# First stage of a two-layer attention kernel: a modulation third in two column halves, products by feature halves, and the shift applied as columns are formed

## The chip, the cores and the metric

The kernel runs on one core of a Trainium2 chip. The metric is the device time of one execution in microseconds (us). Five engines work side by side, each through its own queue in order: TensorE (PE; PEld is its weight load), VectorE (DVE), ScalarE (ACT), GpSimd (POOL) and SyncE (SP), whose queue issues nearly all transfers.

## The reference, cut to what matters

1024 image tokens and 256 context tokens of 1024 features go through two attention layers. What the change touches is the head of the first layer: normalise, modulate by a condition vector, project.

```python
def _modulate(x, cond, norm_g, w_ada, b_ada):
    mod = jax.nn.silu(cond) @ w_ada + b_ada
    shift, scale, gate = jnp.split(mod[:, None, :], 3, axis=-1)
    return rmsnorm(x, norm_g) * (1.0 + scale) + shift, gate

h, gate = _modulate(x, c, norm_g, w_ada, b_ada)
hc, gate_c = _modulate(xc, c_ctx[None, :], norm_g, w_ada, b_ada)
qa, ka, va, qb, kb, vb, g = _split(h @ w_in, EVEN_SPLITS)
```

Everything is float32. The kernel multiplies at that precision by splitting each operand into a high part in a reduced format (fp32r) and the remainder, and adding three products (`mm3`: high x high, high x low, low x high).

## The kernel before, in words

`h` holds the modulated tokens turned to features x tokens: 8 feature tiles (`kt`) of 128 features, 1280 tokens, as a high and a low tile (`hE`). Tokens come in three chunks, `CHUNKS`: 0 to 511 (first tokens), 512 to 1023 (second tokens), 1024 to 1279 (context). The modulation matrix `w_ada_e` has three thirds of 1024 columns: shift (0), scale (1), gate (2). `ada_third` loads a third as eight 128x1024 tiles (`wada`, 512 KB each), multiplies `sil` with them in four column groups into one PSUM tile, copies that (`mrow`), turns it and adds the bias into `modT`.

The first stage, from the kernel's start to the mark "e1":

- The first four token tiles are loaded (`load_x`), normalised (`norm_rows`), turned and copied unscaled (`raw_cols`), while the scale third is loaded and multiplied; `scale_cols` then forms the high and low columns of the first tokens, scaled and not yet shifted. The `issue_after` blocks hold those instructions behind the split of the first projection weight.
- `load_ws` loads four projection tiles (`first = (4, 0, 1, 2)`) one after another through one buffer `wraw` and splits each (ACT the high part, DVE or POOL the remainder).
- `products` multiplies the four weights, one after the other, with the first tokens (`proj_fm`, 24 matmuls of 512 columns each) into four PSUM tiles `early`, and is advanced a little at a time (`Filler`, `FILL_S0`, `FILL_S1`) between the shift third and `cols_scaled` of the second tokens, which are scaled and not yet shifted.
- `bias` multiplies the shift with the four weights, so that `finish` can add it to products of unshifted columns, rotate them (`rope_split`: DVE, POOL, ACT) and store them (`store_hl`).
- `qk_first` makes the same products of the second tokens, again weight by weight, while the context's columns are formed with shift (`h_cols`) and `shift_cols` rebuilds the first tokens' columns with shift.
- `qk_ctx` makes the context's products and those of two further weights, `w5` (`va_part`) and `w3` (`proj_spill`), for the context and the first tokens, while `shift_cols` rebuilds the second tokens' columns.

Behind the mark "e1" come `va_part` and `proj_spill` of the remaining chunk (the second tokens), the split of four weights (`W2`), `va_tm`, and then `v_spill`, whose products fill TensorE while the other thirds are multiplied.

Instructions are traced in the order of the code; a scheduler at compile time sets each engine's own order from that, from the data and from free buffers. At run time every engine goes through its order, and a waiting instruction holds all behind it. `t_ps()` gives two PSUM buffers for turned tiles, `mm_ps()` two, `s_ps()` three, `pv_ps()` one; with `mm_state["wide"]` on, `mm_ps()` also takes from `s_ps()`. Token tiles (`xt`) have six buffers.

Of the kernel before, what the change touches and what calls it, by code (L numbers as in the profile page):

```python
# [18 lines left out]
P = 128  # L19
D = 1024  # L20
# [20 lines left out]
ADA_E1, ADA_BUFS = ((0, 2), (1, 0), (1, 1), (1, 2)), 6  # L41
# [4 lines left out]
H_ACT, FILL_S, W_AHEAD, FILL_S0, FILL_S1, FILL_S2, FILL_S3, FILL_S4, SH_V, HF_BUFS = 2, 1.6, 3, 3.0, 1.4, 8.0, 1.2, 3.0, 3, 2  # L46
# [50 lines left out]
def body(nc, tc, I, out, dbg=None):  # L97
# [325 lines left out]
    def ada_third(wt, name, layer, third, step=1):  # L423
        acc = s_ps()[:, :256]
        for k0 in range(0, NK, step):
            ws_ = []
            for kt in range(k0, k0 + step):
                w = wt.tile([P, D], F32, tag="wada", name="wada", bufs=ADA_BUFS)
                SY.dma_start(w, I[name][kt * P:(kt + 1) * P, third * D:(third + 1) * D])
                ws_.append((kt, w))  # L430
# [18 lines left out]
        else:  # L449
            A.copy(row, acc)  # L450
            if (layer, third) == (0, 1):
                yield 0.0
# [13 lines left out]

    def gate_load(dst, i):
        SY.dma_start(dst, GROW[i:i + 1].to_broadcast([P, D]))

    def norm_rows(tp, xs):  # L470
        n = len(xs)
        ss = tiny.tile([P, n], F32, tag=f"ss{n}", name="ss")
        for i, x in enumerate(xs):
            junk = tp.tile([P, D], BF16, tag="junk", name="junk", bufs=1)
            A.activation(junk, x, AF.Square, accum_out=ss[:, i:i + 1])
        r = rstd_of(ss, n, D)
        for i, x in enumerate(xs):
            V.tensor_scalar(x, x, r[:, i:i + 1], None, ALU.mult)
# [17 lines left out]

    def raw_cols(xns, raw):
        n = len(xns) * P
        for kt in range(NK):
            ps = t_ps()  # L500
            for b, xn in enumerate(xns):
                T_.transpose(ps[:, b * P:(b + 1) * P], xn[:, kt * P:(kt + 1) * P], ident)
            (V.tensor_copy if kt % 2 else A.copy)(raw[:, kt, :n], ps[:, :n])

    def scale_cols(raw, layer, j, c0, n, h):
        for kt in range(NK):
            gs = modT[layer][:, 8 + kt, j:j + 1]
            hi, lo = h[0][:, kt, c0:c0 + n], h[1][:, kt, c0:c0 + n]
            A.activation(hi, raw[:, kt, c0:c0 + n], AF.Identity, scale=gs)
            V.scalar_tensor_tensor(lo, raw[:, kt, c0:c0 + n], gs, f32(hi), ALU.mult, ALU.subtract)  # L510
# [42 lines left out]
    with ExitStack() as st:  # L553
# [3 lines left out]
        sr, sc = ExitStack(), ExitStack()  # L557
        sp = pool(sc, "start", 2, side="left")
        raw0 = pool(sr, "raw0", 1, side="left").tile([P, NK, 512], F32, name="raw0")
# [26 lines left out]
        lo_cycle["engs"] = [V, G]  # L586
        first = (4, 0, 1, 2)
        ws, xs = [], []

        def load_ws():  # L590
            j = len(ws)
            raw = wsp.tile([P, D], F32, tag="raw", name="wraw")
            SY.dma_start(raw, I["w_e"][first[j]])
            a = A.copy(wst[0][:, j], raw)
            v = (G if j % 2 else V).tensor_tensor(wst[1][:, j], raw, f32(wst[0][:, j]), ALU.subtract)
            ws.append([w[:, j:j + 1] for w in wst])
            return a.ins, v.ins

        rows = [load_x(b) for b in range(4)]
        norm_rows(xp, rows)  # L600
        raw_cols(rows, raw0)
        ada = ada_third(sp, "w_ada_e", 0, 1)
        for _ in range(NK + 1):
            next(ada)
        split = load_ws()
        run(ada)
        with tc.issue_after(split[0]), tc.issue_after(split[1]):
            scale_cols(raw0, 0, 0, 0, 512, h)
        for i in range(4):
            if len(ws) < min(i + 1, W_AHEAD):  # L610
                load_ws()
            xs.append(load_x(4 + i))
        sr.close()
        early = [mm_ps(), mm_ps(), s_ps(), pv_ps()]

        def products():
            for j in range(4):
                yield from proj_fm(ws[j], h, 0, 512, ps=early[j])
                yield 1.28

        prods = Filler(products())
        prods(FILL_S0)
        norm_rows(xp, xs)
        cols = cols_scaled(xs, 0, 0, 512, h)
        for i, _ in enumerate(ada_third(sp, "w_ada_e", 0, 0)):
            if i % 2 and len(ws) < 4:
                load_ws()
            prods(FILL_S1)
            next(cols, None)
        run(cols)  # L630
        sc.close()
# [34 lines left out]
        def qk_first():  # L666
            for j in range(4):
                ps = yield from proj_fm(ws[j], h, 512, 512)
                finish(j, ps, 512, 512)
                yield 1.28  # L670
# [9 lines left out]
        def qk_ctx():  # L680
            for j in range(4):
                yield from proj_chunk(tp, ws[j], h, S, L, cs, QK[first[j]])
            for c in (2, 0):
                yield from va_part(c)
                yield from proj_spill(tp, w3, h, CHUNKS[c:c + 1], cs, QK[3])

        mm_state["wide"] = True
        bias()
        prods.drain()
        for j in range(4):  # L690
# [3 lines left out]
        side(FILL_S2)  # L694
# [16 lines left out]
    with ExitStack() as st:  # L711
# [15 lines left out]
        with ExitStack() as sq:  # L727
            tp = pool(sq, "q3", 2, side="left")
            run(va_part(1))
# [879 lines left out]
```

## Time and profile before

| | us |
|---|---|
| median of 3 runs | 1656.78 (1656.08 to 1659.83) |
| the profiled execution | 1659.88 |
| its span in the trace | 1658.1 |
| TensorE busy | 1583.4 of the span |
| DVE, ACT, POOL busy | 1085.6, 777.8, 540.2 |

The profiled execution has 1.8 us outside its span. A matmul's busy time overlaps its neighbour's in the trace, since they are pipelined: what one costs is the distance from its start to the next one's start.

### The profile page before, as it was taken

How to read it: one execution, taken by the hardware profiler on the slowest of the kernel's cores; microseconds unless marked ns; L12 is line 12 of the kernel's file. 1: busy time of each engine (PE TensorE's matmuls, PEld its weight loads, DVE VectorE, ACT ScalarE, POOL GpSimd, SP SyncE). 2: the span in 40 equal slices, each digit the busy share in tenths (PEclk: the TensorE clock that was granted, in tenths of full speed). 3: DMA queues.
4: the chain of work that ended last, by engine and by line, in shares of the span. 5: the costliest groups of instructions: out<-in, count | busy, mean ns of one | idle time of the engine just before them, and what ended most of it. 6: DMA issues, size and time to landing. Idle time of an engine off the chain costs nothing. (4 is left out here: it accounts for less than half of the span.)

```text
span 1658.1 us, 26760 instructions
## 1 busy us (share of the span) xinstructions
PE 1583.4 (95%) x9250; PEld 1330.5 (80%) x9250; DVE 1085.6 (65%) x2954; ACT 777.8 (47%) x1580; POOL 540.2 (33%) x713
## 2 busy tenths in 40 slices
PE   6989999999998999999899999999999999999997
PEld 3677768888877878888677797989888888888886
DVE  4674128878759887887777546343587756665576
ACT  5443006766646566556333323222476655554421
POOL 0365024555444333323333202120243414322211
PEclk9989999999999999999999999999999999999999
DMA  7547663242262333222853623557755436321452
GB/s 287 180 115 247 242 200 119 84 141 90 71 219 96 97 109 113 89 87 77 255 190 114 186 61 105 187 178 240 224 167 174 131 118 196 100 81 64 140 191 83
DMA packets 147231, 242.40 MB, mean 146 GB/s; under 512 B 10236, under 2 KB 93976, under 8 KB 144920
## 3 DMA queue, kind: packets, MB, share of 16 engines
q1 hardware_dynamic: 142184, 227.32, 43.6%
q10 hardware_dynamic: 4576, 11.54, 1.8%
q0 software_dynamic: 336, 1.84, 0.3%
q8 instruction: 73, 1.20, 0.3%
q14 instruction: 62, 0.51, 0.1%
HBM read 162.91 MB, written 77.74 MB: 145 GB/s over the span
## 5 line engine op out<-in xcount | busy, mean ns | idle before, releaser
L304 PE MATMUL mmps<-hE,whi 128*128 128x512 f32 (+1 forms) x408 | 148.7, 364 | 1.3 <-DVE gg L396 1.3
L218 POOL TENSOR_TENSOR wlo<-wraw,whi 128x256 fp32r<-128x256 f32 x120 | 92.4, 803 | 174.0 <-ACT whi L251 168.9
L306 PE MATMUL mmps<-hE,wlo 128*128 128x512 f32 (+1 forms) x408 | 146.4, 359 | 0.0
L305 PE MATMUL mmps<-hE,whi 128*128 128x512 f32 (+1 forms) x408 | 146.3, 359 | 0.0
L914 ACT ACTIVATE sB_t<-sB_t,mB 128x1280 f32<-128x1280 f32 (+1 forms) x80 | 95.5, 1194 | 58.9 <-DVE sB_t L407 49.4
L906 PE MATMUL sps<-kb,qb 128*128 128x512 f32 (+1 forms) x416 | 107.4, 359 | 5.8 <-DVE sB_t L407 3.1
L924 POOL TENSOR_SCALAR sB_t<-sB_t,cB 128x256 f32<-128x256 f32 x84 | 38.6, 479 | 157.9 <-DVE cB L920 76.3
L407 DVE TENSOR_SCALAR_CACHE_REDUCE sB_t<-sps,mB 128x512 f32<-128x512 f32 (+1 forms) x128 | 78.4, 613 | 12.4 <-PE sps L906 9.4
L304 PEld LDWEIGHTS mmps<-hE,whi 128*128 128x128 f32 x408 | 77.3, 190 | 11.4 <-issue 2.1
L306 PEld LDWEIGHTS mmps<-hE,wlo 128*128 128x128 f32 x408 | 77.2, 189 | 10.0 <-issue 0.8
L305 PEld LDWEIGHTS mmps<-hE,whi 128*128 128x128 f32 x408 | 77.2, 189 | 9.2 <-issue 0.8
L906 PEld LDWEIGHTS sps<-kb,qb 128*128 128x128 f32 x416 | 68.8, 189 | 18.3 <-DVE sB_t L407 7.1
L1442 POOL TENSOR_SCALAR sM_t<-sM_t,sM 128x1280 f32<-128x1280 f32 x32 | 43.4, 1357 | 117.5 <-DVE sM L1441 116.6
L218 POOL TENSOR_TENSOR rot<-rot,csE 128x256 f32<-128x256 f32 x52 | 41.3, 814 | 112.1 <-DVE rot L331 108.4
L1340 POOL TENSOR_SCALAR sD_t<-sD_t,sD 128x640 f32<-128x640 f32 (+1 forms) x64 | 50.0, 800 | 81.7 <-DVE sD L1337 49.9
L305 PE MATMUL mmps<-hO,whi 128*128 128x512 f32 (+1 forms) x192 | 74.5, 388 | 1.7 <-POOL hO L214 1.6
L304 PE MATMUL mmps<-hO,whi 128*128 128x512 f32 (+1 forms) x192 | 75.4, 393 | 0.0
L784 ACT ACTIVATE sA_t<-sA_t,mA 128x640 f32<-128x640 f32 (+2 forms) x80 | 59.6, 745 | 31.8 <-DVE sA_t L407 29.2
L306 PE MATMUL mmps<-hO,wlo 128*128 128x512 f32 (+1 forms) x192 | 74.4, 388 | 0.0
L218 POOL TENSOR_TENSOR yl<-o_in,yh 128x256 fp32r<-128x256 f32 x36 | 33.6, 953 | 115.2 <-ACT yh L866 106.6
L221 ACT CAST phm<-tps 128x512 fp32r<-128x512 f32 x80 | 45.6, 583 | 51.4 <-PE tps L1469 51.1
L794 POOL TENSOR_SCALAR sA_t<-sA_t,eA 128x640 f32<-128x640 f32 (+2 forms) x80 | 56.0, 721 | 38.0 <-DVE eA L792 14.7
(435 smaller groups left out, 5210.8 us busy)
## 6 DMA issues: line engine op xcount, KB each, us to landing
wraw<-w_e SPq DMA_DIRECT2D x26, 512.0 KB
wada<-w_ada_e SPq DMA_DIRECT2D x24, 512.0 KB
wada<-w_ada_o SPq DMA_DIRECT2D x24, 512.0 KB
wraw<-w_o SPq DMA_DIRECT2D x22, 512.0 KB
qb<-qk SPq DMA_DIRECT2D x76, 128.0 KB
qd_t<-qd SPq DMA_DIRECT2D x32, 256.0 KB
qk<-hl SPq DMA_DIRECT2D x10, 512.0 KB
vb<-vh SPq DMA_DIRECT2D x10, 512.0 KB
```

Of the source, the lines that this page charges most:

```text
L218: eng.tensor_tensor(out_[:, cs_], a[:, cs_], b[:, cs_], op)
L221: A.copy(dst_hi, src)
L304: T_.matmul(ps, lh, rh, start=first, stop=False)
L305: T_.matmul(ps, lh, rl, start=False, stop=False)
L306: T_.matmul(ps, ll, rh, start=False, stop=last)
L407: V.tensor_scalar(dst, ps, -scale, prev, ALU.mult, ALU.min, accum_out=acc)
L784: A.activation(St[:, :nl + L], St[:, :nl + L], AF.Exp, bias=mx, scale=-1.0, accum_out=ssum[:, i:i + 1])
L794: G.tensor_scalar(Ps[i][:, :nl + L], Ps[i][:, :nl + L], e[:, i:i + 1], 1.0, ALU.mult, ALU.mult)
L906: T_.matmul(ps[:, :n], Q[:, t, hl, i * P:(i + 1) * P], K[:, t, c0:c0 + n], start=hl == 0, stop=hl == 1)
L914: A.activation(St[:, :ncol], St[:, :ncol], AF.Exp, bias=mx, scale=-1.0, accum_out=s0g[:, si:si + 1] if t == 0 else ssum)
L1340: G.tensor_scalar(Ps[i][:, :w_], Ps[i][:, :w_], ssum[:, i:i + 1], 1.0, ALU.mult, ALU.mult)
L1442: G.tensor_scalar(St, St, ssum, 1.0, ALU.mult, ALU.mult)
```

## The change

The scale third becomes two column halves of 512 (`ada_half`), each loaded with four transfers of 512 KB that take two row blocks at once. The first half is asked for before the first two weights, the second behind them. The first tokens are turned straight into scaled columns (`cols_scaled`, with `raw_cols` and `scale_cols` gone), four feature tiles behind each half. The products of the first tokens go by feature tile, weights 0 and 1 together, then weight 2, and weight 3 at the end. Weights are split in two parts each. The second tokens are only normalised in this part; their columns, like the context's, are formed with shift (`h_cols`) once the shift third is there, and their products go by feature tile as the columns come, weights 0 and 1, then 2 and 3, without `bias`. `shift_cols` stays for the first tokens alone. The second tokens' `va_part` and `proj_spill` move into `qk_first`, and the first tokens' behind the mark "e1".

```diff
+    def ada_half(wt, name, layer, third, half):
+        acc = s_ps()[:, :P]
+        c0 = third * D + half * 512
+        src = I[name][:, c0:c0 + 512].rearrange("(k a p) c -> k p a c", a=2, p=P)
+        for k in range(NK // 2):
+            w = wt.tile([P, D], F32, tag="wada", name="wada", bufs=ADA_S).rearrange("p (a c) -> p a c", a=2)
+            SY.dma_start(w, src[k])
...
+        for kt in range(NK):
+            for g in range(4):
+                T_.matmul(acc[32 * g:32 * g + 32, :], sil[:, kt], ws_[kt // 2][:, kt % 2, g * P:(g + 1) * P],
+                          start=kt == 0, stop=kt == NK - 1)
+            yield
...
-        norm_rows(xp, rows)
-        raw_cols(rows, raw0)
-        ada = ada_third(sp, "w_ada_e", 0, 1)
...
-        with tc.issue_after(split[0]), tc.issue_after(split[1]):
-            scale_cols(raw0, 0, 0, 0, 512, h)
...
+        halves = [ada_half(sp, "w_ada_e", 0, 1, i) for i in range(2)]
+        next(halves[0])
+        raws = [ws_raw(0), ws_raw(1)]
+        next(halves[1])
+        norm_rows(xp, rows, on_act=1)
...
+            steps = [((0, 1), (kt,)) for kt in range(4)] + [((2,), (0, 1)), ((2,), (2, 3))]
+            steps += [((0, 1), (kt,)) for kt in range(4, NK)] + [((2,), (4, 5)), ((2,), (6, 7))]
+            steps += [((3,), (kt, kt + 1)) for kt in range(0, NK, 2)]
...
+        ws_split(0, raws[0], V)
+        with tc.issue_after(turned.ins):
+            cols = cols_scaled(rows, 0, 0, 0, h)
...
+        ws_split(2, ws_raw(2), V)
+        xs = [load_x(4), load_x(5)]
+        raws.append(ws_raw(3))
+        tiles = [ada_tile(sp, "w_ada_e", 0, kt, ADA_S) for kt in range(4)]
+        next(prods)
+        run(halves[1])
...
+        run(cols)
+        xs += [load_x(6), load_x(7)]
...
+        tiles += [ada_tile(sp, "w_ada_e", 0, kt, ADA_S) for kt in range(4, NK)]
+        shift_third = ada_third(sp, "w_ada_e", 0, 0, tiles=tiles)
+        squared = norm_rows(xp, xs)
...
+        with tc.issue_after(squared.ins):
+            run(shift_third)
...
         def qk_first():
-            for j in range(4):
-                ps = yield from proj_fm(ws[j], h, 512, 512)
-                finish(j, ps, 512, 512)
-                yield 1.28
+            for js in ((0, 1), (2, 3)):
+                pss = [s_ps() if js[0] == 0 else mm_ps() for _ in js]
+                for kt in range(NK):
...
+            yield from va_part(1)
+            yield from proj_spill(tp, w3, h, CHUNKS[1:2], cs, QK[3])
...
-        mm_state["wide"] = True
-        bias()
-        prods.drain()
-        for j in range(4):
-            finish(j, early[j], 0, 512)
...
+        lo_cycle["engs"] = [V, V, G]
...
+        bias()
+        for i, _ in enumerate(h_cols(tp, xs, 0, 0, 512, h, hf_act=H_ACT)):
+            if i:
+                side(FILL_S)
+        finish(0, early[0], 0, 512)
+        finish(1, early[1], 0, 512)
         norm_rows(xp, xc)
-        for _ in h_cols(xp, xc, 0, 1, S, h, hf_act=H_ACT):
-            side(FILL_S)
-        for _ in shift_cols(xp, 0, 0, 0, 512, h):
-            side(FILL_S3)
+        for i, _ in enumerate(h_cols(tp, xc, 0, 1, S, h, hf_act=H_ACT)):
+            side(FILL_C)
+            if i in (1, 4):
+                j = 2 + i // 4
+                finish(j, early[j], 0, 512)
+        for _ in shift_cols(tp, 0, 0, 0, 512, h):
+            side(FILL_H)
         side.drain()
-        side = Filler(qk_ctx())
-        for _ in shift_cols(xp, 0, 0, 512, 512, h):
-            side(FILL_S4)
-        side.drain()
+        mm_state["wide"] = True
+        run(qk_ctx())
...
-            run(va_part(1))
+            run(va_part(0))
```

## Rows read from the trace of the kernel before

**Rows 1.** The page: span, and busy time by engine.

```profile
span 1658.1 us, 26760 instructions
...
PE 1583.4 (95%) x9250; PEld 1330.5 (80%) x9250; DVE 1085.6 (65%) x2954; ACT 777.8 (47%) x1580; POOL 540.2 (33%) x713
```

**Rows 2.** Windows: start to end, length, busy us (instructions), clock, DMA share, GB/s.

```profile
0.00:28.44 28.44, 14.50 (x99) 6.08 (x99) 9.86 (x32) 10.74 (x19) 0.51 (x5) 1.00 0.80 304
28.44:141.81 113.37, 107.39 (x570) 83.19 (x571) 75.65 (x130) 53.87 (x91) 57.41 (x62) 0.94 0.52 169
141.81:155.63 13.82, 10.94 (x67) 7.28 (x65) 9.12 (x14) 4.87 (x10) 11.41 (x12) 0.88 0.72 243
```

**Rows 3.** Timeline up to the first products: start, us, engine, line, operation.

```profile
13.50 2.74 DVE L478 TENSOR_SCALAR xt<-xt,rsy 128x1024 f32<-128x1024 f32 x4
...
24.73 1.50 PE L433 MATMUL sps<-wada,sil 128*32 128x256 f32 x22
...
27.18 0.17 DVE L461 TENSOR_TENSOR modT<-tps,small 128x16 f32<-128x16 f32 x1 [1.65 <-PE tps L455]
...
28.44 0.50 PE L304 MATMUL mmps<-hE,ws 128*128 128x512 f32 x1 [1.29 <-ACT hE L509]
...
29.58 0.50 PE L305 MATMUL mmps<-hE,ws 128*128 128x512 f32 x1 [0.64 <-DVE hE L510]
```

**Rows 4.** Windows for the transfer rate; the last has 2 KB runs.

```profile
0.00:4.00 4.00, 0.00 (x0) 0.00 (x0) 0.73 (x6) 1.70 (x3) 0.51 (x5) 1.00 0.48 114
4.00:20.00 16.00, 7.83 (x33) 2.33 (x34) 5.30 (x21) 4.91 (x9) 0.00 (x0) 1.00 1.02 404
99.00:101.50 2.50, 2.50 (x13) 2.02 (x12) 1.40 (x2) 1.66 (x4) 1.22 (x3) 1.00 0.59 156
```

**Rows 5.** Windows of one kind of matmul: 512 columns, slow 512, 256 columns.

```profile
70.00:78.00 8.00, 8.00 (x36) 6.46 (x35) 6.71 (x9) 3.08 (x5) 6.65 (x8) 1.00 0.01 2
90.00:94.00 4.00, 4.00 (x11) 3.03 (x11) 3.03 (x4) 0.48 (x1) 2.65 (x3) 0.50 0.44 158
102.00:112.00 10.00, 10.00 (x86) 9.99 (x85) 7.64 (x13) 2.97 (x6) 5.89 (x8) 1.00 0.33 76
```

**Rows 6.** Timeline of TensorE: groups, and the matmul behind each.

```profile
38.08 0.64 PE L433 MATMUL sps<-wada,sil 128*32 128x256 f32 x8
38.65 0.50 PE L306 MATMUL mmps<-hE,ws 128*128 128x512 f32 x1
...
49.65 0.60 PE L517 MATMUL tps<-consts,xt 128*128 128x128 f32 x4
50.00 0.48 PE L306 MATMUL sps<-hE,ws 128*128 128x512 f32 x1
...
59.88 3.87 PE L652 MATMUL tps<-ws,shs 128*2 128x512 f32 x16
...
65.30 1.05 PE L656 MATMUL tps<-ones,brow 2*128 2x2 f32 x8
```

**Rows 7.** TensorE's waits, first 160 us: in total, times, longest.

```profile
PE tps L485 <- ACT hf L491: 2.3, 1, 2.3
...
PE tps L485 <- DVE hf L493: 2.0, 1, 2.0
...
PE sps L304 <- DVE hl L214: 1.0, 1, 1.0
```

**Rows 8.** Groups by line, first 143 us: busy us, mean ns, idle before.

```profile
L218 POOL TENSOR_TENSOR hE<-hf,hE 128x256 fp32r<-128x256 f32 x20 | 18.4, 943 | 9.7 <-ACT hE L530 9.6
...
L529 DVE SCALAR_TENSOR_TENSOR hf<-hE,modT,hE 128x512 f32<-128x512 f32 x16 | 14.1, 885 | 8.3 <-POOL hE L218 7.5 <-POOL hE L214 0.7
...
L521 DVE SCALAR_TENSOR_TENSOR hE<-tps,modT,hE 128x512 fp32r<-128x512 f32 x8 | 5.8, 751 | 6.7 <-ACT hE L520 6.7
```

**Rows 9.** Timeline of TensorE where the projections end and `v_spill` begins.

```profile
141.81 1.03 PE L722 MATMUL tps<-consts,vat 128*128 128x128 f32 x8
...
146.34 0.64 PE L305 MATMUL mmps<-wlo,hE 128*128 128x512 f32 x1 [2.07 <-DVE wlo L214]
```

More of the change, by code (lines that the diff above doesn't have):

```diff
@@ L420, in pv_acc, with ada_third @@
         T_.matmul(pv, vh, pl, start=False, stop=last)
-    def ada_third(wt, name, layer, third, step=1):
+    def ada_third(wt, name, layer, third, step=1, tiles=None):
         acc = s_ps()[:, :256]
@@ L427, in ada_third @@
             for kt in range(k0, k0 + step):
-                w = wt.tile([P, D], F32, tag="wada", name="wada", bufs=ADA_BUFS)
-                SY.dma_start(w, I[name][kt * P:(kt + 1) * P, third * D:(third + 1) * D])
-                ws_.append((kt, w))
+                ws_.append((kt, tiles[kt] if tiles else ada_tile(wt, name, third, kt)))
             for kt, w in ws_:
@@ L584, in load_x, with ws_raw @@
             return x
-        lo_cycle["engs"] = [V, G]
         first = (4, 0, 1, 2)
[L588 to L592, printed above, removed]
+        ws = [[w[:, j:j + 1] for w in wst] for j in range(4)]
+        def ws_raw(j):
+            raw = sp.tile([P, D], F32, tag="raw", name="wraw", bufs=2)
             SY.dma_start(raw, I["w_e"][first[j]])
[L594 to L597, printed above, removed]
@@ L613, in body, with ws_split @@
-        sr.close()
+            return raw
+        def ws_split(j, raw, eng, parts=2):
+            n = D // parts
+            for i in range(parts):
+                cs_ = slice(i * n, (i + 1) * n)
+                A.copy(wst[0][:, j, cs_], raw[:, cs_])
+                tt(eng, wst[1][:, j, cs_], raw[:, cs_], f32(wst[0][:, j, cs_]), ALU.subtract)
+        rows = [load_x(b) for b in range(4)]
+        halves = [ada_half(sp, "w_ada_e", 0, 1, i) for i in range(2)]
+        next(halves[0])
+        raws = [ws_raw(0), ws_raw(1)]
@@ L614, in body @@
+        next(halves[1])
+        norm_rows(xp, rows, on_act=1)
+        for _ in range(NK + 1):
+            next(halves[0])
+        turned = next(halves[0])
         early = [mm_ps(), mm_ps(), s_ps(), pv_ps()]
         def products():
-            for j in range(4):
-                yield from proj_fm(ws[j], h, 0, 512, ps=early[j])
-                yield 1.28
[L621 to L629, printed above, removed]
@@ L630, in body @@
-        run(cols)
+            steps = [((0, 1), (kt,)) for kt in range(4)] + [((2,), (0, 1)), ((2,), (2, 3))]
+            steps += [((0, 1), (kt,)) for kt in range(4, NK)] + [((2,), (4, 5)), ((2,), (6, 7))]
+            steps += [((3,), (kt, kt + 1)) for kt in range(0, NK, 2)]
+            for js, kts in steps:
+                for j in js:
+                    for kt in kts:
+                        ks = slice(kt * P, (kt + 1) * P)
+                        mm3(early[j], ws[j][0][:, 0, ks], ws[j][1][:, 0, ks], h[0][:, kt, :512], h[1][:, kt, :512],
+                            kt == 0, kt == NK - 1)
+                yield
@@ new lines, in body @@
+        prods = products()
+        ws_split(0, raws[0], V)
+        with tc.issue_after(turned.ins):
+            cols = cols_scaled(rows, 0, 0, 0, h)
+            next(cols)
+            ws_split(1, raws[1], G)
+            next(cols)
+            next(prods)
+            next(cols)
+            next(prods)
+            for _ in range(NK // 2):
+                next(halves[1])
+            next(cols)
+            next(prods)
+            for _ in range(NK // 2):
+                next(halves[1])
+            next(halves[1])
+            next(prods)
@@ new lines, in body @@
+        ws_split(2, ws_raw(2), V)
+        xs = [load_x(4), load_x(5)]
+        raws.append(ws_raw(3))
+        tiles = [ada_tile(sp, "w_ada_e", 0, kt, ADA_S) for kt in range(4)]
+        next(prods)
+        run(halves[1])
+        for _ in range(2):
+            next(cols)
+        next(prods)
+        run(cols)
+        xs += [load_x(6), load_x(7)]
+        for _ in range(4):
+            next(prods)
+        ws_split(3, raws[2], G)
+        tiles += [ada_tile(sp, "w_ada_e", 0, kt, ADA_S) for kt in range(4, NK)]
@@ L631, in body @@
+        shift_third = ada_third(sp, "w_ada_e", 0, 0, tiles=tiles)
+        squared = norm_rows(xp, xs)
+        for _ in range(4):
+            next(shift_third)
+        for _ in range(4):
+            next(prods)
+        for _ in range(4):
+            next(shift_third)
+        run(prods)
+        with tc.issue_after(squared.ins):
+            run(shift_third)
         sc.close()
```

81 lines of the change are left out of this document (45 added, 36 removed).

## The prediction

> **What bounds the kernel now.** I read the page first [rows 1]: TensorE is busy for 1583.4 of 1658.1 us, DVE for 1085.6, ACT and POOL for less. So TensorE is the bound nearly everywhere, and the change leaves its count of large products alone: what it can win is time in which TensorE waits, or runs slowly, in the first stage. Next the stage in windows [rows 2]: up to the first product at 28.44 us TensorE is busy for 14.50, much of it slow small matmuls; from there to the last projection at 141.81 it is busy for 107.39 of 113.37 at a mean clock of 0.94; then 13.82 us in which `v_spill` starts, at 0.88.
>
> The timeline [rows 3] shows what the first product waits for. The rows are normalised from 13.50 on, the scale third's last matmuls start only at 24.73, the modulation is written at 27.18, the first product starts at 28.44 and the second at 29.58, behind the low columns. Transfers [rows 4] move 114 GB/s in the first 4 us and 404 GB/s from 4 to 20, with the engines full: 0.46 MB by 4 us and 0.404 MB each us from then on. Small tables are 0.23 MB, four token tiles 2.10: with a whole third (4.19) that is 6.52 MB, landed by 19 us. So before lost 8 us between the last byte and the modulation.
>
> For 28.44 to 141.81 I count the work at full clock. A 512-column matmul costs 0.23 us, a slow one 0.42, a 256-column one 0.12 [rows 5] (records in the window less the one or two that started ahead of its edge). There are 288 of the first kind in the code (96 early, 96 of the second tokens, 96 of `w5` and `w3`), 66.5 us, and 144 of 256 columns, 17.1. The modulation costs 0.57 for a row block (38.08 to 38.65) [rows 6], 4.6 for the shift third; four turned tiles 0.35 [rows 6], 4.2 for the 48 of second tokens and context; the bias 3.7 and about 1.0 [rows 6]. The sum is 97.1, so 113.4 - 97.1 = 16.3 us are lost. Of it 5.3 are waits for columns and stores [rows 7], about 3.7 the matmuls at 1.2 GHz that follow them (some 19 at 0.42 instead of 0.23), 1.6 the same at the first products, and about 3.6 the eight switches to a row block of the shift third and back (rows 38.08 and 38.65 are one of them); the rest is small.
>
> **The change part by part.** *First product.* The first half-third needs 0.23 + 2.10 + 2.10 = 4.43 MB: 4 + (4.43 - 0.46) / 0.404 = 13.8 us. Its source has runs of 2 KB where it had 4. The nearest row for such runs is that of stores (99 to 101.5) [rows 4]: 156 GB/s at a share of 0.59 is 264 when busy, which would make 2.10 MB cost 8.0 us instead of 5.2. Bounds 0 and 2.8; I take 0.3, since these stores use 64 partitions and write, and a load of 128 resembles the 404 row more. The rows are then the later side: three of four scalings on DVE are 3 x 0.69 = 2.1 behind 13.50, 15.6 [rows 3]; the copy, turn and modulation lie beside that, except two DVE steps of 0.17. From the modulation to the first product took 28.44 - 27.18 = 1.3 us, and now four turned tiles of 0.35 stand between; the second product is 1.1 later [rows 3]. The first weight (0.52 MB behind the half) lands at 15.1 and its two part splits lie on ACT and DVE in front of the columns, in the shadow of the turned tiles for the most part. So products run from about 17.5 us (15.6 + 0.35 + 1.3 + 0.3): 10.9 earlier.
>
> *What moves behind it.* Before, these 10.9 us held work that now comes after the first product: 28 of 32 turned tiles, 2.5 us, and the second half-third, whose 8 row blocks have half the columns; between half and all of 0.57 each, 2.3 to 4.6, I take 3.4. Net 10.9 - 5.9 = +5.0.
>
> *Pace of the first columns.* One feature tile costs DVE 0.75 (0.751 mean) [rows 8] and ACT about as much, and gives TensorE six matmuls and four turned tiles, 1.39 + 0.35 = 1.74. TensorE stays the slower one, so the steps should not starve, given the operands. Behind the first half SP asks for two weights, the second half (landed 4 + (7.57 - 0.46)/0.404 = 21.6), weight 2, two token tiles, weight 3, four tiles of the shift third, then the last two token tiles, which wait in SP's queue for buffers that the first tokens' last turn frees, and behind them the other four shift tiles. By bytes these land at 22.9, 25.5, 26.8, 32, 34.6 and 39.8. TensorE, from 17.5 us, needs the second half at about 22.5, weight 2 at 25, the shift's first half at 36, its second at 42. All but weight 2 (whose buffer and split come late) have slack; I take 1.5 us of waits, bounds 0 and 4. A late buffer would hold shift tiles, tables, context and two weights behind it on SP; the price is then that of the wait alone, until the slack of 2 us is gone. The ramp at 1.2 GHz costs 1.6 as before.
>
> *Switches.* The shift third goes in two blocks and the second half-third in two: four switches, 1.8, where there were eight, 3.6. Turned tiles between matmuls were there before too; for their eight more switches I take 0.8.
>
> *The join.* `bias` holds both buffers for turned tiles, and the second tokens' columns need the shift and those buffers. From a turned tile to a low column is ACT, ACT or DVE, then POOL in two pieces of 0.94 [rows 8], some 3.5 us, against which only the last products of the first tokens stand. Bounds 0 and 5; I take 2.0, since `finish` of tiles that are done waits behind the columns and not ahead of them.
>
> *Forming with the shift.* Gone: eight `shift_cols` steps of the second tokens (DVE 0.885 [rows 8], ACT, POOL) and four bias additions on ACT. The columns cost one step more than a scaled column did. Finishing eight QK tiles is spread over columns of second tokens, context and first tokens instead of standing in a row, but by my count of operations DVE and POOL still have nearly as much work there as TensorE. Before, waits and the slow clock in this part cost 5.3 + 3.7 = 9.0 [rows 5, 7]; bounds 0 and 9, I take 3.0, a third: of the three waits two stood between four finished tiles in a row, and that row is gone.
>
> *`v_spill`.* Its low weights arrived late: TensorE waited 2.07 [rows 9] and ran at 0.88. The last cover ahead of it is 11 us of products as before, only of other tokens. I take no change; bounds a gain of 4.7 (2.07 of wait, the rest slow clock) and a loss of 4.
>
> *Sum.* +5.0 for the start. The losses behind it were 16.3, of them 2.1 small ones, and become 1.6 + 1.5 + 1.8 + 0.8 + 2.0 + 3.0 + 2.1 = 12.8: +3.5. Together 8.5 us. The profiled execution's 1659.88 becomes 1651.4; it stands 3.1 above the median, so the predicted median is 1656.78 - 8.5 = 1648 us.
>
> **A rule against this change.** In the window of 90 to 94 us the granted clock is 0.50, that is 1.2 of 2.4 GHz, behind two waits of 2.3 and 2.0 us [rows 5, 7]. The Trainium skill, "TensorE: Matmul & The Clock Gate", section "HAM oscillation", says that a loop which waits for an operand at each tile of the contraction falls back to the slow clock every time, and advises all tiles of the contraction in one go. The products of this change go feature tile by feature tile. By this rule they would stay slow; by rows 8 the wait between them is covered.
>
> **Rivals.** *Slow steps.* If each step waits for its columns long enough that TensorE stays at 1.2 GHz, the 96 matmuls of weights 0 and 1 cost 0.42 instead of 0.23, 18.2 us more: against the 8.5: 10 slower than before, 1666. It decides from about 45 slow matmuls on (8.5 / 0.19). For it: the clock of 0.50 at 90 to 94 us behind two waits. Against: DVE's 0.75 against TensorE's 1.74. 8%. *Start won, middle lost.* DVE and POOL pace the columns as before, losses stay at 16.3 and the join of 2 to 5 comes on top: 5.0 - 3.5 = 1.5 us, 1655. For it: POOL's 0.94 for 256 columns and DVE's waits for POOL [rows 8]. 17%. *Weights set the time.* `v_spill` starts when its four weights are split, whenever the projections end [rows 9]; if their transfers, queued on SP behind stores of results, do not move, nothing is won: 1657. 6%. *All losses go.* Start +6.1 with the cheap half, the losses at 1.6 + 1.8 + 0.8 + 1 = 5.2, so +11.1, and `v_spill`'s late weights (4.7 at most) may go too: 17 to 22, 1637. 17%. *The forecast*, 4 to 16 us: 52%.
>
> **How the numbers follow.** A measurement of this kernel tells about 0.2%, 3.3 us. Faster: 52 + 17 + 8 of the 17 = 77%. Same: 8 of the 17 and 5 of the 6 = 13%. Slower: 8 and the rest = 10%. The range 1637 to 1656 leaves out the slow steps, the weights, part of the last good case and a little of the middle one, about 2 in 10. The likeliest case's own range is 1641 to 1653.
>
> **What would show it.** First product at 17 to 19 us (before 28.44); the last projection ahead of `v_spill` at 130 to 136 (before 141.81); the granted clock at 1.00 from 22 us on, against 0.50 at 90 to 94; the waits for `hf` gone or below 2 us. I would be wrong if the steps show a clock of 0.50, if TensorE waits for shift tiles at 40 us, or if the stretch behind "e1" gives back what came before it.

## The result

The changed kernel takes 1669.45 us (median of 6 runs, 1666.72 to 1673.02) where the kernel before took 1656.45 beside it: a ratio of 1.0076, 95% interval 1.0059 to 1.0094. By that ratio it is 12.6 us slower. Forecast were 1648 us, some 8.5 us faster, with a range of 1637 to 1656. The profiled execution took 1672.99 us.

The page of the changed kernel has TensorE busy for 2.6 us more than [rows 1], in a span 13.1 us longer.

```profile
span 1671.2 us, 26864 instructions
...
PE 1586.0 (95%) x9314; PEld 1339.6 (80%) x9314; DVE 1070.5 (64%) x2944; ACT 773.4 (46%) x1574; POOL 536.1 (32%) x713
```

The windows cut the first stage of the changed kernel at the first product, behind the last product of the first tokens, at the first product with a low column of the second tokens, just ahead of the first rotation on DVE, at 112 us, at the end of the projections and at the first `vh`, which is the first result of `v_spill` (columns as in [rows 2]).

```profile
0.00:19.22 19.22, 6.43 (x74) 4.22 (x74) 6.83 (x29) 9.49 (x17) 0.52 (x5) 1.00 0.91 336
19.22:53.08 33.86, 33.86 (x251) 25.14 (x250) 12.14 (x28) 14.75 (x26) 5.64 (x8) 1.00 0.88 334
53.08:64.73 11.65, 7.64 (x42) 3.96 (x40) 6.11 (x21) 5.12 (x10) 2.73 (x2) 0.97 0.07 16
64.73:84.00 19.27, 18.52 (x77) 14.37 (x78) 5.28 (x8) 8.49 (x13) 8.19 (x11) 0.84 0.13 46
84.00:112.00 28.00, 24.03 (x121) 20.86 (x120) 26.29 (x43) 10.34 (x19) 19.83 (x22) 0.82 0.33 95
112.00:149.58 37.58, 32.79 (x175) 27.97 (x175) 14.73 (x24) 10.07 (x20) 17.36 (x22) 0.95 0.57 158
149.58:166.36 16.78, 11.13 (x56) 7.60 (x58) 10.31 (x14) 6.32 (x11) 8.00 (x6) 0.80 0.71 226
```

The first two lines are what was hoped for: the first product at 19.22 us instead of 28.44 [rows 2], then 34 us without a gap. The rest is where it went wrong. From 64.73 to 84.00 DVE, the third engine column, is busy for 5.28 of 19.27 us; from 84 to 112 for 26.29 of 28.00. TensorE's mean clock is 0.84 in the first of these two windows, where it is still busy for 18.52 of 19.27 us, and 0.82 in the second, where it also waits (24.03 of 28.00). Lost time, counted as in the prediction (length less the matmuls' cost at full clock), is 2.1, 4.9, 4.9, 8.7, 7.0 and 8.7 us in the six windows behind the first product. Before it was 5.6 up to 68.7 (which includes the bias), 10.0 from there to 141.81 and 5.0 up to its first `vh` at 157.14. A few matmul records are missing in each, so these are good to about 1 us.

TensorE's timeline in the changed kernel: the bias (59.88 before [rows 6]), the first products of the second tokens, and the start of `v_spill` (146.34 before, behind one wait of 2.07 [rows 9]).

```profile
54.23 3.85 PE L710 MATMUL tps<-ws,shs 128*2 128x512 f32 x16 [0.77 <-DVE rv L207]
...
61.25 0.73 PE L304 MATMUL sps<-hE,ws 128*128 128x512 f32 x2 [0.43 <-ACT hE L525]
...
64.73 0.79 PE L305 MATMUL sps<-hE,ws 128*128 128x512 f32 x1 [2.15 <-POOL hE L218]
...
154.86 0.74 PE L304 MATMUL mmps<-whi,hE 128*128 128x512 f32 x2 [1.48 <-ACT whi L251]
...
158.28 0.76 PE L305 MATMUL mmps<-wlo,hE 128*128 128x512 f32 x1 [2.68 <-DVE wlo L214]
```

DVE's timeline in the changed kernel shows the pile being made.

```profile
64.02 0.80 DVE L530 TENSOR_SCALAR hf<-tps,modT 128x512 f32<-128x512 f32 x1
...
69.78 0.81 DVE L530 TENSOR_SCALAR hf<-tps,modT 128x512 f32<-128x512 f32 x1 [4.25 <-ACT hE L525]
...
76.24 0.81 DVE L530 TENSOR_SCALAR hf<-tps,modT 128x512 f32<-128x512 f32 x1 [4.92 <-ACT hE L525]
...
82.36 0.81 DVE L530 TENSOR_SCALAR hf<-tps,modT 128x512 f32<-128x512 f32 x1 [4.59 <-ACT hE L525]
...
85.00 0.74 DVE L331 STREAM_SHUFFLE rot<-sps 128x512 f32<-128x512 f32 x1
...
89.03 0.75 DVE L331 STREAM_SHUFFLE rot<-qf 128x512 f32<-128x512 f32 x1
```

The four `hf` steps come one per 6 us. Each is released by ScalarE's `hE` step on the same turned tile, and that step waits for TensorE, which turns a tile only after the products that `side(FILL_S)` deals out in between. The `qf` of the two tiles that `finish(0)` and `finish(1)` rotate were there early. ScalarE's timeline shows both:

```profile
62.42 0.69 ACT L719 ACTIVATE qf<-mmps,qb 128x512 f32<-128x512 f32 x1
...
65.39 0.68 ACT L719 ACTIVATE qf<-mmps,qb 128x512 f32<-128x512 f32 x1
68.97 0.78 ACT L525 ACTIVATE hE<-tps,modT 128x512 fp32r<-128x512 f32 x1 [2.91 <-PE tps L522]
```

Yet their rotation starts at 89.03, since it stands behind the last `hf` in DVE's queue, and behind the rotations of the second tokens' first two tiles (`rot<-sps`, from 85.00). The Trainium skill, "PSUM — Partial Sum Buffer", section "Engine vs sequencer instructions", says that these engines' queues are strictly first in, first out; the 24 us between 65 and 89, most of them idle on DVE, agree.

TensorE's waits in the changed kernel up to 170 us (in total, times, longest; compare [rows 7]): the one for `hf` is down to 1.2, as forecast, and others stand in its place.

```profile
PE sps L305 <- POOL hE L218: 2.9, 2, 2.1
PE sps L305 <- DVE hE L214: 2.8, 2, 2.1
PE mmps L305 <- DVE wlo L214: 2.7, 1, 2.7
PE mmps L304 <- DVE hl L214: 2.5, 1, 2.5
...
PE tps L522 <- DVE hf L530: 1.2, 1, 1.2
```

What hangs on the finished tiles is seen in SP's timeline of the changed kernel: twelve stores of `hl` hold its queue from 104.32 to 132.6, and only behind them `v_spill`'s weights are asked for.

```profile
104.32 28.32 SPq L342 DMA_DIRECT2D qa<-hl  x12
...
133.89 1.36 SPq L247 DMA_DIRECT2D wraw<-w_e  x2
```

Before, the first of the four was asked for at 121.20, 20.6 us ahead of the last projection's end; now it is 15.7.

### The profile page after: what moved, and what is told of

Its sections match the earlier page's. It is cut to its first block, busy times and chain, and to the rows that moved or that the text cites. A ratio compares the mean times of both kernels' runs of the same rounds, so it can differ in the third digit from the quotient of the medians.

```text
span 1671.2 us, 26864 instructions
## 1 busy us (share of the span) xinstructions
PE 1586.0 (95%) x9314; PEld 1339.6 (80%) x9314; DVE 1070.5 (64%) x2944; ACT 773.4 (46%) x1574; POOL 536.1 (32%) x713
## 5 line engine op out<-in xcount | busy, mean ns | idle before, releaser
L304 PE MATMUL mmps<-hE,whi 128*128 128x512 f32 (+1 forms) x424 | 156.0, 368 | 4.5 <-DVE hl L214 2.5
L306 PE MATMUL mmps<-hE,wlo 128*128 128x512 f32 (+1 forms) x424 | 153.3, 361 | 0.0
L305 PE MATMUL mmps<-hE,whi 128*128 128x512 f32 (+1 forms) x424 | 153.1, 361 | 0.0
L304 PEld LDWEIGHTS mmps<-hE,whi 128*128 128x128 f32 x424 | 80.9, 191 | 16.0 <-DVE hl L214 2.9
L306 PEld LDWEIGHTS mmps<-hE,wlo 128*128 128x128 f32 x424 | 80.7, 190 | 10.8 <-issue 0.8
L305 PEld LDWEIGHTS mmps<-hE,whi 128*128 128x128 f32 x424 | 80.6, 190 | 9.9 <-issue 0.8
L304 PE MATMUL mmps<-hO,whi 128*128 128x512 f32 (+1 forms) x200 | 78.5, 392 | 0.0
L305 PE MATMUL mmps<-hO,whi 128*128 128x512 f32 (+1 forms) x200 | 77.4, 387 | 0.0
```

The source lines that it names most:

```text
L304: T_.matmul(ps, lh, rh, start=first, stop=False)
L305: T_.matmul(ps, lh, rl, start=False, stop=False)
L306: T_.matmul(ps, ll, rh, start=False, stop=last)
```

## The experiments

The table has, for each kernel, three times of its one profile, the end of the projections (where `vat` is turned), the first scores (the first product of `ka`) and the time from there to the end of the span, and the ratio to the kernel before, beside which it ran. The kernel before took 1656.45 us (median) beside the changed kernel and 1659.8 to 1661.2 beside the others, so ratios are compared and not times. Behind the first stage the instructions are those of before, in almost the same order.

| kernel | projections end | first scores | scores to end | ratio (95% interval) |
|---|---|---|---|---|
| before | 141.8 | 252.1 | 1406.0 | |
| changed | 149.6 | 262.8 | 1408.4 | 1.0076 (1.0059 to 1.0094) |
| e1 new start, old middle | 140.4 | 249.1 | 1408.7 | 0.9999 (0.9984 to 1.0015) |
| e2 old start, new middle | 155.5 | 262.4 | 1407.8 | 1.0047 (1.0030 to 1.0064) |
| e3 two tiles finished early | 140.6 | 250.6 | 1407.2 | 1.0017 (0.9998 to 1.0035) |
| e4 old chunk order | 145.3 | 253.2 | 1411.7 | 1.0022 (1.0003 to 1.0041) |
| e8 both repairs | 142.8 | 252.3 | 1412.4 | 1.0036 (1.0023 to 1.0048) |
| before, no rotation | 132.6 | 242.5 | 1406.1 | 0.9934 (0.9919 to 0.9949) |
| e1, no rotation | 127.4 | 238.4 | 1409.6 | 0.9949 (0.9931 to 0.9967) |
| changed, no rotation | 135.9 | 249.9 | 1413.9 | 1.0013 (0.9998 to 1.0028) |
| changed, count aligned | 149.1 | 261.9 | 1411.4 | 1.0066 (1.0048 to 1.0084) |
| e8, count aligned | 142.6 | 252.4 | 1414.8 | 1.0047 (1.0029 to 1.0066) |
| e9 shift early, aligned | 144.3 | 253.8 | 1412.2 | 1.0034 (1.0020 to 1.0048) |
| e12 new start, context first | 143.1 | 252.6 | 1412.7 | 1.0041 (1.0025 to 1.0056) |
| e13 old start, context first | 145.7 | 258.1 | 1403.8 | 1.0012 (0.9998 to 1.0026) |
| e14 before, delayed | 139.0 | 250.7 | 1412.4 | 1.0030 (1.0013 to 1.0047) |
| e15 before, ring swapped | 140.4 | 250.3 | 1406.7 | 1.0000 (0.9988 to 1.0013) |
| e16 e1, ring back | 139.5 | 248.7 | 1410.6 | 0.9997 (0.9985 to 1.0009) |
| e17 e3, ring back | 142.4 | 251.1 | 1408.4 | 1.0016 (1.0002 to 1.0030) |

Three of these (before, e14, e15) have one and the same first stage: its end varies from 139.0 to 141.8 and the first scores from 250.3 to 252.1, and e14's 250.7 has work of some 2.5 us in it that the others lack. So differences under about 3 us in a single profile tell nothing there.

**Which half costs.** e1 keeps the new start and puts back everything behind it; e2 does the reverse.

```diff
-            for js in ((0, 1), (2, 3)):          # e1; e2 the other way round
...
+            for j in range(4):
+                ps = yield from proj_fm(ws[j], h, 512, 512)
+                finish(j, ps, 512, 512)
+                yield 1.28
```

> The changed start (scale third in halves, products of the first tokens by feature tile) with the middle of before: second tokens scaled without shift beside the last products, shift added to them later, products weight by weight, chunks of the two further weights in the old order. Theory M (the loss is made in the middle, where columns formed with the shift stand on TensorE's path and eight tiles are finished in one pile on DVE): the start's 7 to 9 us stay won, 1647 to 1651 against before, and the stretch from the last early product to v_spill loses about 10 us as before instead of 25. Rival S (the start's gain is only work put off, or its transfers cost later): 1655 or more. Rival W (v_spill waits for its weights whatever stands ahead): 1655 to 1658, with the wait ahead of v_spill grown.

> The start of before with the changed middle (second tokens' and context's columns formed with the shift, products by feature tile, other order of chunks). Theory M: slower than before by the middle's 15 us and v_spill's 4, less what the second tokens' columns no longer cost in the start (about 3): 1668 to 1677. Rival S: the middle is neutral, 1655 to 1662.

The new start alone is worth nothing that can be measured; the new middle alone costs 7.8 us (4.9 to 10.6), and both together 12.6 (9.8 to 15.6). These two intervals overlap, so the 4.8 between them need not be a loss of its own. At the first scores e2 is as late (262.4) as the changed kernel (262.8). So the loss is the middle's, and with the new middle the start's lead is gone by the first scores. Two parts of that middle were not tried alone: the products by feature tile, and the low parts of weights and finished tiles, of which DVE gets two in three (`[V, V, G]`) where it got every second.

**What of the middle.** e3 finishes the first two tiles between the turned columns of the second tokens; e4 puts chunk 1 of `w5` and `w3` back behind "e1" and chunk 0 ahead of it.

```diff
             if i:
                 side(FILL_S)
-        finish(0, early[0], 0, 512)
-        finish(1, early[1], 0, 512)
+            if i in (1, 4):
+                finish(i // 4, early[i // 4], 0, 512)
```

> The changed kernel with the first two early tiles finished inside the loop that forms the second tokens' columns, at its second and fifth step, instead of behind it. Theory M in its second half (DVE stands idle at 64 to 84 us and is then full to 112, so the context's columns come late): the stretch 94 to 110 loses 3 or less instead of 8.5, and the time falls by 4 to 7 us to 1662 to 1666. Rival (the chain from turned tile to low column sets the pace, wherever finishing stands): no change, or slower, because the finishing steps now stand between columns on DVE, ACT and POOL.

> The changed kernel with only the order of the two further weights' products put back: first tokens' and context's chunks behind the context's products, the second tokens' behind the mark. Theory W2 (v_spill's weights come late because the four first weights are needed until 126 us and the SP queue holds the loads behind stores): the weights are asked for some 10 us earlier, the loss ahead of v_spill falls from 9.3 to 5, 3 to 5 us faster than the changed kernel. Rival: the context's products then stand directly behind late columns and wait longer, same time or slower.

e3 moves two calls and wins back 12.3 us at the first scores, and 9.8 us of the whole time (1.0017 for 1.0076; the intervals do not overlap). In its DVE timeline the first early tile is rotated from 62.46 on instead of 89.03:

```profile
61.73 0.80 DVE L530 TENSOR_SCALAR hf<-tps,modT 128x512 f32<-128x512 f32 x1
...
62.46 0.73 DVE L331 STREAM_SHUFFLE rot<-qf 128x512 f32<-128x512 f32 x1
```

and its windows have DVE's work spread and TensorE at a better clock between 84 and 112 (0.94 for 0.82):

```profile
64.00:84.00 20.00, 17.66 (x80) 13.76 (x79) 12.97 (x17) 9.86 (x15) 13.20 (x15) 0.92 0.26 79
84.00:112.00 28.00, 23.62 (x112) 19.61 (x111) 24.29 (x39) 10.12 (x20) 19.67 (x23) 0.94 0.43 111
```

e4 wins 9.6 us at the first scores. Its projections end 5 us later than e3's, and from there to the first `vh` it takes 12.4 us instead of 16.8 (e3 13.2). Both ask for `v_spill`'s weights 8 us sooner than the changed kernel does. e8 has both edits:

> The changed kernel with both repairs: the first two tiles finished between the turned columns of the second tokens, and chunk 1 of value and gate projected ahead of the context again. If the two recover different losses (10 and 9 us of 12.6), their sum goes beyond the loss: 1648 to 1653 us, a ratio of about 0.996. If they recover the same one (the weights of the next part asked for late), it stays where each was alone: 1658 to 1662 us, a ratio of 1.001 to 1.002.

They do not add up: 252.3 us at the first scores, between the two, and a ratio of 1.0036, above both within the intervals. So the two recover one and the same loss in the main. That it is the lateness of `v_spill`'s weights is not shown. SP's timelines of e3, e4 and e8, in this order, have the first of these weights asked for at the times below; e8 asks 13 us sooner than the others and is no faster:

```profile
125.43 0.85 SPq L247 DMA_DIRECT2D wraw<-w_e  x1
...
125.47 1.38 SPq L247 DMA_DIRECT2D wraw<-w_e  x2
...
112.57 0.33 SPq L247 DMA_DIRECT2D wraw<-w_e  x1
```

**Is it the rotation's work?** Three kernels leave the rotation out of eight tiles (shuffle, GpSimd's multiplication, DVE's multiplication and addition).

> The kernel before, with the rotation (the shuffle, the two multiplications and the addition) left out for the first stage's eight tiles of Q and K, so that VectorE and GpSimd have less to do behind the shift; its output is another. It is the yardstick of the two that follow. If VectorE and GpSimd set the pace behind the shift, it is 3 to 9 us faster than before (the loss of 8 us behind 81 goes); if TensorE does, it is the same within 2 us.

> The new start with the old middle, again without the rotation in the eight tiles. If VectorE and GpSimd behind the shift ate the 8 us that the new start gains, the gain reappears: 5 to 9 us faster than the old start without the rotation. If the gain was lost to something else (the transfers, the shift known no earlier), the two are the same within 2 us, as they were with the rotation.

> The changed kernel, again without the rotation in the eight tiles. If the pile of work on VectorE (rotations queued behind the forming of the second tokens) is what costs 12.6 us, most of it goes: at most 4 us over the old kernel without the rotation, and the loss between 94 and 110 falls below 3 us. If the loss comes from the order of the chunks and from the late weights of the next part, some 9 of the 12.6 us stay.

The windows from 80 to 100 us of the kernel before, of it without the rotation, and of e1 without it:

```profile
80.00:100.00 20.00, 15.66 (x58) 11.64 (x57) 15.00 (x23) 8.47 (x16) 13.58 (x15) 0.74 0.55 157
```

```profile
80.00:100.00 20.00, 19.55 (x118) 16.65 (x117) 9.87 (x16) 12.04 (x23) 9.55 (x12) 1.00 0.56 160
```

```profile
80.00:100.00 20.00, 19.42 (x140) 17.93 (x139) 11.22 (x16) 10.59 (x20) 11.77 (x14) 1.00 0.51 151
```

Without the rotations TensorE stays busy, at full clock; with them it is busy for 15.66 us at 0.74. So in the old kernel too DVE and GpSimd set the pace behind the shift, and take some 10 us. My theory that they eat the new start's lead is half right. With the rotation the two starts end their projections within the scatter (139.0 to 141.8 against 139.5 and 140.4); without it the new start is 5.2 us ahead there (127.4 against 132.6), as expected. But it then waits for the next weights, which the earlier end has caught up with:

```profile
127.40 1.03 PE L791 MATMUL tps<-consts,vat 128*128 128x128 f32 x8
...
133.20 0.77 PE L306 MATMUL mmps<-wlo,hE 128*128 128x512 f32 x1 [3.34 <-DVE wlo L215]
```

At the first scores 4.1 us are left, at the end nothing. And the changed kernel without the rotation is still 7.3 us late at the first scores, against 10.7 with it: the rotations' work is about a third of the lateness there. Of the rest, 3.3 us are there at the end of the projections and 3.7 more up to the first `vh`. Over the whole time nothing goes: the pair without the rotation lies 13.1 us apart (1.0013 against 0.9934), the pair with it 12.6. The expectation (4 us at most) failed. So the rotations' work doesn't explain the 12.6 us. What e3 moves, and the kernel without the rotation leaves late, is the place of finishing in the queue. SP's first store of a finished tile in the changed kernel, in it without the rotation, and in e3:

```profile
90.38 0.62 SPq L345 DMA_DIRECT2D qk<-hl  x1
...
83.33 0.63 SPq L349 DMA_DIRECT2D qk<-hl  x1
...
73.72 0.63 SPq L345 DMA_DIRECT2D qk<-hl  x1
```

e12 and e13 form the context's columns between the finishes of the first four tiles instead of behind all four, and have ScalarE make all `hf` copies (`hf_act=1`), so they change two things at once.

```diff
-        for j in range(4):
-            finish(j, early[j], 0, 512)
...
+        cols = h_cols(tp, xc, 0, 1, S, h, hf_act=1)
+        for j in range(4):
+            next(cols)
+            next(cols)
+            finish(j, early[j], 0, 512)
+            side(4.0)
```

> New start and old middle, but the context's columns are formed between the finishes of the first four tiles instead of behind all four, and their `hf` copies are made by ScalarE. If VectorE's queue behind the shift eats the start's lead, the waits of TensorE for `hf` (4.8 us) go, the loss of 14 us between 81 and 120 falls below 7, the first scores come at 241 to 245 us instead of 249.1, and the ratio is 0.995 to 0.997. If the work of VectorE and GpSimd as such is the bound there, whatever its order, the first scores stay within 2 us of 249.

> The kernel before with the same reorder. It separates the start's lead from the reorder's own gain: if the queue ate the lead, this gains less than the new start does, its first scores come 3 to 7 us later than those of the run beside it. If the reorder gains the same with either start, the lead of 3 us between them stays as it was.

Both are later at the first scores, by 3.5 and 6.0 us. So it isn't that this one order was bad: with the work that DVE and GpSimd have there, another order moves the waits and may add to them. The new start was 5.5 us ahead in this pair, and behind at the end.

**Is the join a loss of its own?** e9 asks for the shift's third ahead of the second tokens and puts the bias ahead of the last products.

```diff
-        xs = [load_x(4), load_x(5)]
         raws.append(ws_raw(3))
-        tiles = [ada_tile(sp, "w_ada_e", 0, kt, ADA_S) for kt in range(4)]
+        tiles = [ada_tile(sp, "w_ada_e", 0, kt, ADA_S) for kt in range(NK)]
+        xs = [load_x(4), load_x(5)]
```

> As the one with both repairs and the count aligned, and the shift third is asked for ahead of the second tokens and multiplied, with the bias, between the last products of the first tokens, so that the join has no chain of shift, bias and turning in a row. If the join (some 6 us of lost TensorE time from 53 to 66, and 4 behind it) is a loss of its own, the shift is known near 42 us instead of 53, the first scores come 4 to 8 us earlier than with both repairs alone (244 to 248 us), and the ratio is about 0.996. If VectorE and GpSimd set the pace from there whatever the join, the first scores come within 2 us of 252 and the ratio is that of the run beside it.

It also scales the second tokens' rows later (from 53.34 on, for 43.95). Its bias starts at 47.06 instead of 54.23 and no product waits for it, yet the first scores come 1.4 us later than with both repairs and the count aligned. What the join no longer loses is lost a little further on. DVE is full there, and has the rotations of the first tiles, the context's row scaling and a weight's low part ahead of its first `hf`, which comes no sooner than in the changed kernel (64.02):

```profile
60.00:64.00 4.00, 1.84 (x8) 1.42 (x9) 4.00 (x6) 3.38 (x6) 3.10 (x4) 0.94 0.00 0
64.00:68.00 4.00, 3.16 (x11) 2.17 (x10) 3.90 (x9) 0.95 (x3) 1.19 (x2) 0.50 0.46 147
68.00:72.00 4.00, 4.00 (x14) 3.10 (x14) 3.90 (x9) 1.43 (x2) 2.50 (x4) 0.70 0.84 246
```

```profile
65.13 0.80 DVE L530 TENSOR_SCALAR hf<-tps,modT 128x512 f32<-128x512 f32 x1
```

**The later stages.** From the first scores on the kernels with the old start take 1403.8 to 1407.8 us, and e14, which has the program of before there, 1412.4; those with the new start take 1407.2 to 1414.8. Two causes of a difference were tried and fell: the count that deals out PSUM buffers, which the new stage leaves two short, and the ring of the two turned-tile buffers, which it leaves swapped.

```diff
     mark("e1")
     mm_state["wide"] = False
+    mm_state["n"] += 2                                 # count aligned
...
     mark("A")
+    T_.transpose(t_ps()[:, :P], ident, ident)          # e15, e16, e17
```

> The changed kernel with one line more: behind the first stage the count that deals out the PSUM buffers is put forward by the two takes that the new stage has fewer, so that every later stage has the buffers and the order of instructions of the kernel before. If the buffers' order costs time in the later stages, the time from the first scores (product of `ka`) to the end goes from 1408.4 to 1406 us and the ratio from 1.0076 to about 1.006; if not, both stay within 1 us, and 1.0076 stays. The lateness of the first scores, 10.7 us, stays in either case.

> Both repairs (two tiles finished early, old order of the chunks) with the count aligned. The two repairs alone had the first scores at 252.3 us, as the kernel before, but 1412.5 us from there to the end instead of 1406.0. If the count is what cost those 6 us, this ties with the kernel before: ratio 0.999 to 1.001. If it isn't, the ratio stays near 1.0036.

> The kernel before with one turned block more, of the identity (0.1 us, output unused), ahead of the attention, so that the ring of the two turned-tile buffers is in the phase that the new start leaves it in. If the phase costs the later stages their time, the time from the first scores rises from 1406 to some 1410 us and the ratio is 1.002 to 1.003. If it doesn't, the ratio is 0.9995 to 1.0005.

> New start and old middle, with the same block, so that the ring is in the phase of the kernel before. If the phase is what ate the lead, the time from the first scores falls from 1408.7 to about 1406 us and the ratio from 0.9999 to about 0.998. If not, the ratio stays within 0.0005 of 0.9999.

> The changed kernel with two tiles finished early (1.0017), with the same block. If the phase counts, the ratio falls to about 0.999; if not, it stays at 1.001 to 1.0025.

None moved the ratio beyond its interval. The windows from the first scores to the end, of the kernel before and of e8 with the count aligned, hold the same 7938 matmuls:

```profile
252.10:1658.10 1406.00, 1355.33 (x7938) 1165.73 (x7937) 974.90 (x2749) 699.24 (x1446) 459.78 (x619) 0.99 0.43 134
```

```profile
252.40:1667.20 1414.80, 1359.85 (x7938) 1170.88 (x7937) 973.89 (x2749) 699.04 (x1446) 460.27 (x619) 0.99 0.43 134
```

Of the 8.8 us more, 4.5 are matmuls that take longer, and 4.3 gaps between them. In windows of 4 us the granted clock falls below 0.97 at three places in the first (5.2 us lost) and at five in the second (12.0), leaving out the last 10 us, where it falls in every kernel. Most places are the same in all kernels, some 290, 520, 540, 770 and 1312 us behind the first scores, and in each kernel some of them show a fall and others none. e14 puts 28 turned blocks into the kernel before and changes nothing else:

> The kernel before with 28 turned 128-column blocks of the identity more (some 2.5 us of TensorE, output unused) ahead of the first scores, so that the later stages begin a little later. If their time were fixed, the end moves by 2.5 us and the time from first scores to the end stays 1406 us. If it depends on where their waits fall in time, it changes by a multiple of about 1.7 us (what one dip of the granted clock costs in these profiles: the sums are 3.4, 5.2, 6.8, 8.5, 10.2 and 12.0 us), to 1403 to 1415 us.

TensorE's timeline has these blocks ahead of the first scores (250.7):

```profile
219.13 2.73 PE L752 MATMUL tps<-consts 128*128 128x128 f32 x23
...
222.90 0.77 PE L752 MATMUL tps<-consts 128*128 128x128 f32 x5
```

So from the first scores on it has the work of before and nothing more, and yet its profile takes 6.4 us more there, with other dips: none at 520, one more at 1312, 6.8 us in all. Its whole time is 5.0 us longer, but the interval, 2.2 to 7.8, does not exclude the 2.5 alone. That the later start moved the dips is not shown, since one program's own runs differ as much: the 117 runs of the kernel before beside the experiments took 1654.45 to 1667.23 us, at mean granted clocks of 0.994 to 0.988. Nor do the dips put the kernels in order: e1 without the rotation lost 3.4 us in them and took 1409.6 from the first scores on, e15 lost 6.8 and took 1406.7. The difference of the two starts in the later stages stays open.

No version that computes the whole was faster than the kernel before: e1 and e16 tie with it.

## Why the prediction was wrong

*First product*: nearly right. Forecast were about 17.5 us, and 17 to 19 as the sign; measured are 19.22. The runs of 2 KB were no brake (395 GB/s from 4 to 15.65 us). But the prediction had the scaled rows as the later side, and they were ready at 15.95 (13.87 + 2.08). Later was the modulation, written at 18.00: the half's last row blocks started at 15.65, behind a transfer that the sum had landed by 14.1. Below are a window up to there and lines of DVE's and TensorE's timelines.

```profile
4.00:15.65 11.65, 3.25 (x49) 1.85 (x49) 4.27 (x19) 5.75 (x9) 0.00 (x0) 1.00 1.03 395
...
13.87 2.08 DVE L514 TENSOR_SCALAR xt<-xt,rsy 128x1024 f32<-128x1024 f32 x3
...
15.65 1.08 PE L480 MATMUL sps<-wada,sil 128*32 128x128 f32 x16 [0.25 <-DMA wada<-w_ada_e]
...
17.83 0.17 DVE L497 SCALAR_TENSOR_TENSOR modT<-modT,small 128x8 f32<-128x8 f32 x1
```

*Pace of the first columns* and *Switches*: right, or better. Behind the first product 2.1 us are lost where 5.6 were, no shift tile is waited for at 40 us, and at 53.08 the kernel is some 8 us ahead of before with the same work (68.7 less 4.9 for the bias and 2.8 for the 32 turned tiles, which are still to come). The sum so far had about 5. The rival *Slow steps* fell: from 22 to 52 us the changed kernel's clock is 1.00.

```profile
22.00:52.00 30.00, 30.00 (x240) 22.25 (x239) 10.66 (x26) 12.26 (x22) 3.39 (x5) 1.00 0.88 335
```

The rule of the Trainium skill that was set against the change ("TensorE: Matmul & The Clock Gate", "HAM oscillation") did not come into play there, since no tile was waited for. Further on a column was waited for: from 64 to 68 us, behind the wait of 2.15 us, the clock is 0.51.

*The join*: its bounds were 0 and 5 and I took 2.0; 4.9 were lost. e9 showed that this is no price of its own, but the first part of the next.

*Forming with the shift* is the step that failed. I took 3.0 us, with 9 as the bound, since the row of four finished tiles was gone; measured are 4.9 + 8.7 + 7.0 = 20.6 us to the end of the projections, small losses included, twice the 10.0 of before. The mistake was to look at the amount of work ("DVE and POOL still have nearly as much work there as TensorE") and not at when it may run. Before, DVE turned out the second tokens' columns under the early products and was free for rotations when the shift came. In the change the same engine has next to nothing to do from 64.73 to 84.00, since each `hf` waits for a turned tile and the rotations stand behind it, and has everything to do from then on. e3 shows that this order is most of the price: two calls moved ahead give back 9.8 of the 12.6 us. I had named the order ("`finish` of tiles that are done waits behind the columns and not ahead of them") and booked it as a gain.

*`v_spill`*: no change was taken, with 4 as the bound of the loss; 8.7 us are lost where 5.0 were. The weights wait on SP behind stores of the late `hl`; e3 and e4 ask for them 8 us sooner and take 12.4 to 13.2 us instead of 16.8 from the projections' end to the first `vh`. That was the rival *Weights set the time*, with its sign turned: I gave it 6% and no loss.

The rival nearest to the result was *Start won, middle lost* (17%, 1655): its mechanism is what happened, but it kept the losses of before and added the join, where they grew by some 15. And one assumption under the whole sum failed: that what the start gains reaches the end. e1 and e16 have their first scores 1 to 3 us ahead of before and e15, no more than the scatter, and tie at the end (0.9999 and 0.9997).

## What to carry to other kernels

A start that runs sooner is worth what the next engine in line can use of it: before moving work behind a result that comes late, write down for each in-order queue what stands ahead of what, and when the first of it may run. An engine that is two thirds busy on average can be the bound for 28 us if its work is bunched; moving two calls ahead in its queue was worth 12 us at the first scores. And take a first-stage gain to the end by experiment, since the later stages give or take several us of their own.

## What the runs showed beyond that

The later stages of one and the same program order took 1404 to 1415 us, in part by whether the waits at some eight places were followed by a stretch at 1.2 GHz; the 117 runs of the kernel before spread over 13 us, the faster ones mostly at the higher mean clock. DVE's addition of the rotated half, 128x512, took 0.69 us where GpSimd stood still (e1 at 92.55) and 1.20 beside GpSimd's multiplications (at 83.76). Not every addition that meets GpSimd's work is slowed (0.67 in the kernel before at 79.57), but most are, so that a stretch in which both are busy is longer than the count of its operations says.
